# Reading the moving columns of the projections' products backward, with the activations' tiles shifted by 64, 128 and 192 bytes against the weights

## The chip, the cores and the metric

The kernel runs on one core of one Trainium2 chip. The metric is the device time of one execution in microseconds; for the kernel before it is the median of three runs. Names of engines follow the profile: PE is TensorE's matmul row, PEld its weight loads, DVE VectorE, ACT ScalarE, POOL GpSimd, SP the engine that issues most transfers.

## The reference, cut to what matters

Two layers of a hybrid block on 512 tokens of width 1024. Nearly all of the arithmetic is float32 matrix products:

```python
h = rms_norm(x, g_pre_mix);  proj = h @ w_in            # 1024 -> 7752 columns, split in q, k, v, ...
y_a = dsa_attention(q, k, v, qi, ki, wi)                # top-128 selection of keys, 8 heads
y_b = rg_lru(conv(xr), ...) * gelu(gr)
y_c = chunked_spatial_gating(gelu(zu), rms_norm(gelu(zv)), w_spatial, b_spatial)
merged = sum_n sigmoid(gate_logits_n) * (ys_n @ w_branch_n)
x = x + rms_norm(merged @ w_out)
f = square(relu(rms_norm(x) @ w_ffn_up)) @ w_ffn_down;  x = x + rms_norm(f)
ple = (p_i @ w_ple) * sigmoid(x @ w_ple_gate);          x = x + rms_norm(ple)
```

## The kernel before, in words

Activations lie transposed: channels on the 128 partitions, 512 tokens along a row, so that a tile has 512 float32 columns (2048 bytes a partition) and `D_MODEL` is eight tiles. To keep float32 precision each operand is split into a high and a low part of type float32r, and a product is the sum of three matmuls: high weights by high x, low weights by high x, high weights by low x (`mm3`, L296 to L299). A matmul of this kind loads 128 weight columns (the stationary operand, read from `wh` or `wl`) and then streams the moving columns (`xh`, `xl`, or the tiles `K`, `V`, `A`, `B`) through the array into a PSUM bank. In a profile's row `ps<-xh,wh` the first name behind the arrow is the moving operand and the second the weights.

`gemm` (L301) runs `mm3` over the contraction's tiles, so that one output tile of 1024 channels takes 24 matmuls. `gemm_arriving` (L338) is the same for stretches in which the moving tiles are still being made; its matmuls are at L355. `gemm_halves` (L323) calls `gemm` on halves of 256 columns. The other matmuls call TensorE directly and are not touched by the change: `tokens` (L589), the indexer's and the attention's (L657, L661, L671, L958), the float32 transposes through `ident` (L162, L433, L630, L944) and the sums of squares (L407).

The weights of one output tile come in one transfer of 512 KB into `wr`, ACT casts them into `wh` (L242), DVE subtracts to get `wl` (L243). Engines run their instructions in the order in which the Python program writes them; side chains (the indexer's selection, the recurrence, the attention's softmax) are woven in between by a model clock, `tick`, that counts planned microseconds of products.

Where tiles lie: a pool hands out addresses in the order in which its tags first appear, and `LEAD` shifts the first big tile. In the built program every tile that is named here starts at a multiple of 2048 bytes of its partition: `xh`, `xl`, `K`, `V`, `A`, `B`, `M`, `wh`, `wl` and `tmp` alike. A block of 128 weight columns is 512 bytes. So all moving and all weight reads of these products start at 0 modulo 256 bytes. `ident` is the one big moving operand that doesn't: it starts at 64 modulo 256.

Of the kernel before, what the change touches and what calls it, by code (L numbers as in the profile page):

```python
# [8 lines left out]
F32 = mybir.dt.float32  # L9
F32R = mybir.dt.float32r  # L10
# [9 lines left out]
KT = 8  # L20
# [30 lines left out]
def hybrid_block_kernel(ctx, tc, xT, pT, pos, vec, bsp, freq, w_in, w_tok, w_lru, w_sp, w_br, w_out, w_up, w_dn, w_ple, w_gate, out, depth=DEPTH, dbg=None):  # L51
    nc = tc.nc
    V, A, G, PE = nc.vector, nc.scalar, nc.gpsimd, nc.tensor

    cp = ctx.enter_context(tc.tile_pool(name="cp", bufs=1))
# [7 lines left out]
    def nm(p):  # L63
        uid[0] += 1
        return f"{p}_{uid[0]}"

    def tmp(dt=F32):
        return tp.tile([128, S], dt, tag="tmp", name=nm("tmp"), bufs=NTMP)
# [4 lines left out]
    def bank():  # L73
        return pp.tile([128, 512], F32, tag="ps", name=nm("ps"), bufs=8)

    def slot(tag, dt=F32, big=False):
        return cp.tile([128, 4, S] if big else [128, S], dt, tag=tag, name=nm(tag))
# [5 lines left out]
    def width(r):  # L83
        return r.stop - r.start
# [146 lines left out]
    def prep():  # L231
        i = nprep[0]
        nprep[0] += 1
        key, src = order[i]
        raw = wp.tile([128, 1024], F32, tag="wr", name=nm("wr"), bufs=3)
        nc.sync.dma_start(raw, src)
        if key[0] == "sp":
            r3 = raw.rearrange("p (g t) -> p g t", g=8)
            G.affine_select(out=r3, in_=r3, compare_op=ALU.is_ge, fill=0.0, base=0, pattern=[[0, 8], [1, 128]], channel_multiplier=-1)
        hi = wp.tile([128, 1024], F32R, tag="wh", name=nm("wh"), bufs=NWB)  # L240
        lo = wp.tile([128, 1024], F32R, tag="wl", name=nm("wl"), bufs=NWB)
        A.copy(hi, raw)  # L242
        V.tensor_sub(lo, raw, f32v(hi))  # L243
        prepared[key] = (hi, lo)

    def getw(key, ahead=LA):
        assert order[nget[0]][0] == key, (order[nget[0]][0], key)
        nget[0] += 1
        while nprep[0] < min(nget[0] + ahead, len(order)):
            prep()  # L250
        return prepared.pop(key)
# [33 lines left out]
    def tick(us):  # L285
        clk[0] += us
        run_later()
        run_tasks()
# [4 lines left out]
            tick(0.3)  # L293


    def mm3(ps, wh, wl, xh, xl, start, stop):  # L296
        PE.matmul(ps, wh, xh, start=start, stop=False)  # L297
        PE.matmul(ps, wl, xh, start=False, stop=False)  # L298
        PE.matmul(ps, wh, xl, start=False, stop=stop)  # L299

    def gemm(ps, w, xs, kk, c0=0, st=None, r=FULL):  # L301

# [7 lines left out]
    @contextmanager  # L310
    def ordered(last):

        cur = nc.cur_bb
        n0 = len(cur.bb.instructions)
        yield
        for i in cur.bb.instructions[n0:]:
            if i.engine in last:
                tc.add_manual_dep(i, last[i.engine], mybir.DependencyInfo(mybir.DependencyClass.NoSync, mybir.DependencyReason.DATA), reason="ordered")
            last[i.engine] = i.name
# [14 lines left out]
    def gemm_arriving(keys, xs, source, ranges, arrived=None, lag=LAG, tail=TAIL):  # L334


        n = len(keys)
        ws = [getw(key, 0) for key in keys[:-1]]  # L338
        pss = [bank() for _ in keys]
        last = {}  # L340
        for r in ranges:
            gen = source(r)
            for k in range(KT):
                with ordered(last):
                    next(gen)
                    todo = [(o, k) for o in range(len(ws))]
                    if len(ws) < n and k == lag:
                        ws.append(getw(keys[-1], 0))
                        todo += [(n - 1, q) for q in range(k + 1)]
                    if r is ranges[-1] and k >= KT - tail:  # L350
                        todo = [] if k < KT - 1 else [(o, q) for o in range(n) for q in range(KT - tail, KT)]
                    for i, (o, q) in enumerate(todo):
                        h3, l3 = [v.rearrange("p (k c) -> p k c", k=KT) for v in ws[o]]
                        for m in range(3):
                            PE.matmul(pss[o][:, r], (h3, l3, h3)[m][:, q], xs[q][m // 2][:, r], start=q == 0 and m == 0, stop=q == KT - 1 and m == 2)  # L355
                        if r is ranges[-1] and q == KT - 1 and o < n - 1:
                            prep()
                tick(0.65 * len(todo) * width(r) / S)
            if arrived is not None:
                arrived(r)  # L360
        while nprep[0] < nget[0] + LA:
            prep()
        return pss
# [84 lines left out]
    class Norm:  # L448
# [16 lines left out]
        def source(self, r):  # L465
            while r.start not in self.gens:
                tick(0.1)
            return self.gens[r.start]

    XS = [(slot(f"xh{k}", F32R), slot(f"xl{k}", F32R)) for k in range(KT)]  # L470

    def x_tiles(r, xs, g=None, st=None, ys=None, bc=None, gp=None, on_g=()):

        def updated(d):
            if ys is not None and d < KT:
                if gp is None:
                    V.tensor_mul(ys[d][:, r], ys[d][:, r], bc)
                else:  # L480
                    V.scalar_tensor_tensor(ys[d][:, r], ys[d][:, r], gp[:, d:d + 1], bc, op0=ALU.mult, op1=ALU.mult)
                (G if d in on_g else V).tensor_add(X[d][:, r], X[d][:, r], ys[d][:, r])  # L482

        updated(0)
        for d in range(KT):
            x = X[d][:, r]
            if xs is not None:
                hi, lo = [v[:, r] for v in xs[d]]
                if g is None:
                    A.copy(hi, x)  # L490
                else:
                    A.activation(hi, x, AF.Copy, scale=g[:, d:d + 1])  # L492
                if st is not None:
                    st.square(x, r)
            updated(d + 1)
            if st is not None:
                st.accumulate(r)
            if xs is not None:
                if g is None:
                    V.tensor_sub(lo, x, f32v(hi))  # L500
                else:
                    V.scalar_tensor_tensor(lo, x, g[:, d:d + 1], f32v(hi), op0=ALU.mult, op1=ALU.subtract)  # L502
            yield d
# [28 lines left out]
    for l in range(depth):  # L532
# [6 lines left out]
        if l == 0:  # L539
            st = Stats()  # L540

            def gen():
                tiles = x_tiles(FULL, XS, vc[:, V_PRE:V_PRE + 8], st)
                for k in range(KT):
                    first_parts(k)
                    yield next(tiles)
# [5 lines left out]
        rt = st.rt  # L552
        first = gemm_arriving([("in", l, f"xr{j}") for j in range(3)], XS, norm.source if l else lambda r: gen0, HALVES if l else (FULL,), st.row(D, R), 0, TAIL if l else 1)

        def proj(name, ahead=LA):
            ps = bank()
            gemm(ps, getw(("in", l, name), ahead), XS, KT)
            return ps
# [19 lines left out]
        def tokens(n, fn):  # L578
# [3 lines left out]
            for t0 in (0, 2):  # L582
                pss = [bank(), bank()]
                for k in range(KT):
                    wh, wl = [v[:, k % 2] for v in ws[k // 2]]
                    for t, ps in enumerate(pss, t0):
                        xh, xl = [v[:, t * 128:(t + 1) * 128] for v in XS[k]]
                        for i, (x, w) in enumerate(((xh, wh), (xl, wh), (xh, wl))):
# [13 lines left out]
        for j in range(4):  # L602
            ps = first[j]
# [7 lines left out]
            xh, xl = slot(f"B{j}", F32R), slot(f"B{4 + j}", F32R)  # L611
# [5 lines left out]
        ps = proj("ki")  # L617
# [28 lines left out]
        for j in range(4):  # L646
            ps = proj(f"qi{j}")
# [103 lines left out]
        for j in range(4):  # L751
            ps = proj(f"zu{j}")
# [16 lines left out]
        for j in range(4):  # L769
# [3 lines left out]
            for hf in range(2):  # L773
                ps = bank()
# [4 lines left out]
                for s in range(2):  # L779
                    r = slice(64 * s, 64 * s + 64)  # L780
# [55 lines left out]
        for j in range(4):  # L836
# [3 lines left out]
            xc, xh, xl = XC[j]  # L840
# [3 lines left out]
            r, i = tmp(), tmp()  # L844
# [165 lines left out]
        for j in range(4):  # L1010
            f = rope(proj(f"q{j}"))
            q2, ql = (slot(f"A{j}", F32R), slot(f"A{4 + j}", F32R)), tmp(F32R)
            for s in range(2):
                r, other = slice(64 * s, 64 * s + 64), slice(64 - 64 * s, 128 - 64 * s)
# [15 lines left out]
        for d in range(8):  # L1030
            if d % 2 == 0:
                w = getw(("br", l, 0, d // 2))
# [10 lines left out]
        def out_evac(d, r, ps):  # L1043
            st.add(ps, r)
            A.activation(Y[d][:, r], ps, AF.Copy, scale=col(V_POST + d))

        for d in range(5):
            ps = bank()
            gemm(ps, getw(("out", l, d)), M, KT)
            out_evac(d, FULL, ps)  # L1050
        norm = Norm(st, D, lambda r, bc: x_tiles(r, XS, vc[:, V_FFN:V_FFN + 8], st2, Y, bc, on_g=(1, 3, 5)))
        gemm_halves([("out", l, d) for d in (5, 6, 7)], M, lambda i, r, ps: out_evac(5 + i, r, ps), norm.complete)


        R = cp.tile([128, S], F32, tag="R", name=nm("R"))
        first = gemm_arriving([("up", l, 0, i) for i in range(4)], XS, norm.source, HALVES, st2.row(D, R))
        ps = bank()
        gemm(ps, getw(("up", l, 0, 4)), XS, KT)
# [51 lines left out]
        for c in range(2):  # L1110
            w = getw(("ple", l, c), ahead=1)
            if c == 1:
                bc = st3.rstd_bc()
            for i in range(4):
                ps = bank()
# [14 lines left out]
        for d in range(5):  # L1130
            if d < 4:
                ps = first[d]
            else:
                ps = bank()
# [95 lines left out]
```

## Time and profile before

| | |
|---|---|
| median of 3 runs (lowest to highest) | 1858.88 us (1858.13 to 1859.21) |
| the profiled execution's own time | 1859.11 us |
| its span, first to last instruction | 1857.4 us |
| PE busy | 1804.0 us, 97% of the span, 8798 matmuls |
| PEld busy | 1507.9 us, 81% |
| DVE, ACT, POOL busy | 1161.0, 800.9, 361.3 us |
| DMA | 167.77 MB, mean 90 GB/s |
| granted TensorE clock, mean | 0.99 |

A matmul's end is modelled in the profile and overlaps the next one, so that the pitch from start to start, not the duration in a row, tells what a matmul costs.

### The profile page before, as it was taken

Reading aid. Unit: us, or ns where it says so; the run is one execution under the profiler, and the core shown is the slowest. Engines: PE = TensorE matmul, PEld = TensorE weight load, DVE = VectorE, ACT = ScalarE, POOL = GpSimd, SP = SyncE. Lnnn points to the kernel's source line nnn. Section 1 sums busy time; section 2 is a strip of 40 time slices with the busy share of each in tenths; the row PEclk is TensorE's granted clock in tenths of the full one; section 3 lists DMA queues with packets and bytes.
Section 4 is the critical chain, followed back from the end, with each engine's and each line's share of the span. In section 5 each row is a group of like instructions: output and inputs, shape, how many; then the busy total and the mean of one; then the engine's idle time right before and its main releaser. Section 6 shows DMA issues by size and latency. Waiting matters only on the chain.

```text
span 1857.4 us, 22874 instructions
## 1 busy us (share of the span) xinstructions
PE 1804.0 (97%) x8798; PEld 1507.9 (81%) x8798; DVE 1161.0 (63%) x1939; ACT 800.9 (43%) x1292; POOL 361.3 (19%) x292
## 2 busy tenths in 40 slices
PE   8899999999999999999998999999999999999997
PEld 7787777888888888888887877877888888888886
DVE  6689986666386253533685999866563852545355
ACT  5466435564353231323554572455544432222233
POOL 3513212210140000003354141222003200000033
PEclk9999999999999999999999999999999999999998
DMA  5122222222223222232212122221222222222321
GB/s 172 63 91 90 87 97 84 76 78 82 80 91 103 100 93 102 91 114 91 89 60 97 66 93 92 102 80 69 91 80 91 91 91 102 92 101 94 111 80 58
DMA packets 49678, 167.77 MB, mean 90 GB/s; under 512 B 6048, under 2 KB 8864, under 8 KB 49568
## 3 DMA queue, kind: packets, MB, share of 16 engines
q1 hardware_dynamic: 47376, 163.64, 25.7%
q10 hardware_dynamic: 2192, 2.67, 0.4%
q8 instruction: 69, 1.13, 0.2%
q14 instruction: 41, 0.34, 0.1%
HBM read 164.19 MB, written 2.10 MB: 90 GB/s over the span
## 4 chain that ended last, share of the span: by engine, by line
PE 72%; DVE 14%; POOL 5%; issue 4%; ACT 4%; DMA 0%; SPq 0%; POOLq 0%; DVEq 0%; ACTq 0%
PE ps L297 20%; PE ps L299 20%; PE ps L298 20%; PE ps L589 4%; PE ps L355 4%; DVE wl L243 2%; DVE tmp L706 2%; DVE m L704 2%; POOL tmp L574 1%; POOL tmp L575 1%; PE ps L958 1%; POOL sacc L397 1%; POOL X L482 1%; PE ps L671 1%; DVE tmp L781 1%
## 5 line engine op out<-in xcount | busy, mean ns | idle before, releaser
L242 ACT CAST wh<-wr 128x1024 fp32r<-128x1024 f32 x303 | 316.7, 1049 | 453.2 <-PE ps L299 369.2
L243 DVE TENSOR_TENSOR wl<-wr,wh 128x1024 fp32r<-128x1024 f32 x303 | 386.0, 1278 | 190.7 <-ACT wh L242 189.9
L297 PE MATMUL ps<-xh,wh 128*128 128x512 f32 (+1 forms) x1296 | 502.2, 388 | 0.0
L298 PE MATMUL ps<-xh,wl 128*128 128x512 f32 (+1 forms) x1296 | 495.1, 382 | 3.0 <-DVE wl L243 3.0
L299 PE MATMUL ps<-xl,wh 128*128 128x512 f32 (+1 forms) x1296 | 495.4, 382 | 0.0
L397 POOL TENSOR_TENSOR sacc<-sacc,tmp 128x256 f32<-128x256 f32 (+1 forms) x99 | 109.7, 1109 | 893.7 <-issue 584.5
L299 PEld LDWEIGHTS ps<-xl,wh 128*128 128x128 f32 x1296 | 243.7, 188 | 48.2
L298 PEld LDWEIGHTS ps<-xh,wl 128*128 128x128 f32 x1296 | 244.0, 188 | 46.9 <-DVE wl L243 3.8
L297 PEld LDWEIGHTS ps<-xh,wh 128*128 128x128 f32 x1296 | 243.8, 188 | 45.5 <-issue 1.9
L299 PE MATMUL ps<-V,wh 128*128 128x512 f32 (+1 forms) x528 | 195.5, 370 | 0.0
L297 PE MATMUL ps<-K,wh 128*128 128x512 f32 (+1 forms) x432 | 158.2, 366 | 0.0
L298 PE MATMUL ps<-K,wl 128*128 128x512 f32 (+1 forms) x432 | 157.9, 365 | 0.0
L299 PE MATMUL ps<-B,wh 128*128 128x512 f32 x336 | 131.0, 390 | 0.0
L297 PE MATMUL ps<-A,wh 128*128 128x512 f32 x320 | 125.0, 391 | 0.0
L298 PE MATMUL ps<-A,wl 128*128 128x512 f32 x320 | 124.6, 389 | 0.0
L1089 DVE TENSOR_TENSOR M<-M,ps 128x512 f32<-128x512 f32 x48 | 33.0, 688 | 141.4 <-PE ps L299 141.4
L299 PEld LDWEIGHTS ps<-V,wh 128*128 128x128 f32 x528 | 99.5, 188 | 16.8
L1077 DVE TENSOR_TENSOR tmp<-ps,R 128x512 f32<-128x512 f32 x64 | 43.9, 691 | 108.4 <-PE ps L299 108.4
L355 PE MATMUL ps<-xl,wh 128*128 128x256 f32 (+1 forms) x264 | 88.2, 334 | 7.7 <-DVE xl L502 6.9
L297 PEld LDWEIGHTS ps<-K,wh 128*128 128x128 f32 x432 | 81.5, 189 | 13.2
L298 PEld LDWEIGHTS ps<-K,wl 128*128 128x128 f32 x432 | 81.5, 189 | 13.1
L355 PE MATMUL ps<-xh,wh 128*128 128x256 f32 (+1 forms) x264 | 86.5, 328 | 1.0 <-ACT xh L492 1.0
(237 smaller groups left out, 2738.5 us busy)
## 6 DMA issues: line engine op xcount, KB each, us to landing
wr<-in_w_in_dram SPq DMA_DIRECT2D x95, 512.0 KB, 3.2
wr<-in_w_up_dram SPq DMA_DIRECT2D x64, 512.0 KB, 3.2
wr<-in_w_dn_dram SPq DMA_DIRECT2D x64, 512.0 KB, 3.2
wr<-in_w_br_dram SPq DMA_DIRECT2D x24, 512.0 KB, 3.2
wr<-in_w_tok_dram SPq DMA_DIRECT2D x16, 512.0 KB, 3.2
wr<-in_w_out_dram SPq DMA_DIRECT2D x16, 512.0 KB, 3.2
wr<-in_w_gate_dram SPq DMA_DIRECT2D x16, 512.0 KB, 3.2
X<-in_xT_dram SPq DMA_DIRECT2D x8, 256.0 KB, 5.2
```

Source lines behind the costliest of these rows:

```text
L242: A.copy(hi, raw)
L243: V.tensor_sub(lo, raw, f32v(hi))
L297: PE.matmul(ps, wh, xh, start=start, stop=False)
L298: PE.matmul(ps, wl, xh, start=False, stop=False)
L299: PE.matmul(ps, wh, xl, start=False, stop=stop)
L355: PE.matmul(pss[o][:, r], (h3, l3, h3)[m][:, q], xs[q][m // 2][:, r], start=q == 0 and m == 0, stop=q == KT - 1 and m == 2)
L397: G.tensor_add(sacc[:, r], sacc[:, r], self.q[r.start, r.stop])
L589: PE.matmul(ps, x, w, start=k == 0 and i == 0, stop=k == KT - 1 and i == 2)
L704: V.max(m8, (sc if r == 0 else wk)[:, :n])
L706: V.match_replace(wk[:, :n], m8, (sc if r == 0 else wk)[:, :n], -3.0e38)
L1077: V.tensor_mul(t, ps, R)
L1089: V.tensor_add(F[d], F[d], ps)
```

## The change

A new helper `mm` hands TensorE both the moving operand and the output with a column step of -1, so that the last column is streamed first and lands in the last column of the bank: the same product in the same place. `mm3` and the matmuls of `gemm_arriving` call it. And `gap` puts four unused pieces of 64 bytes into the pool that holds the activations, and calls `slot` early for K, V, A and B so that they stand together. In the built program `xh` and `xl` then start at 64 modulo 256 bytes, K and V at 128, A and B at 192; `wh`, `wl`, `tmp`, `M` and `R` stay at 0.

```diff
+    def mm(ps, w, x, start, stop):
+
+        PE.matmul(ps[:, ::-1], w, x[:, ::-1], start=start, stop=stop)
+
     def mm3(ps, wh, wl, xh, xl, start, stop):
-        PE.matmul(ps, wh, xh, start=start, stop=False)
-        PE.matmul(ps, wl, xh, start=False, stop=False)
-        PE.matmul(ps, wh, xl, start=False, stop=stop)
+        mm(ps, wh, xh, start, False)
+        mm(ps, wl, xh, False, False)
+        mm(ps, wh, xl, False, stop)
...
-                            PE.matmul(pss[o][:, r], (h3, l3, h3)[m][:, q], xs[q][m // 2][:, r], start=q == 0 and m == 0, stop=q == KT - 1 and m == 2)
+                            mm(pss[o][:, r], (h3, l3, h3)[m][:, q], xs[q][m // 2][:, r], q == 0 and m == 0, q == KT - 1 and m == 2)
...
+    GAPS = (64, 64, 64, 64)
+
+    def gap(i):
+        if GAPS[i]:
+            cp.tile([128, GAPS[i] // 4], F32, tag=f"gap{i}", name=f"gap{i}")
+
+    gap(0)
     XS = [(slot(f"xh{k}", F32R), slot(f"xl{k}", F32R)) for k in range(KT)]
+    gap(1)
+    for n in ("K0", "K1", "V0", "V1"):
+        slot(n, F32R, True)
+    gap(2)
+    for n in range(8):
+        slot(f"A{n}", F32R)
+        slot(f"B{n}", F32R)
+    gap(3)
```

No engine's instructions change their order. What differs in the built program are waits on PE: 241 of its instructions wait for PE's own semaphore, where 90 did, because the first matmul into a bank now names the earlier matmul that last wrote it. On PE, at the start of an output tile of `w_out` in the first layer (`ps` is the bank, `K` and `V` the merged activations, the numbers behind the names are those of buffers), the kernel before has this order:

```order
L297 MATMUL ps_4263<-K_826_4057,wh_4142 128x512
L298 MATMUL ps_4263<-K_826_4057,wl_4143 128x512
L299 MATMUL ps_4263<-V_828_4059,wh_4142 128x512
L297 MATMUL ps_4298<-K_825_4056,wh_4182 128x512
L298 MATMUL ps_4298<-K_825_4056,wl_4183 128x512
L299 MATMUL ps_4298<-V_827_4058,wh_4182 128x512
```

and the changed kernel, at the same place, this:

```order
L298 MATMUL ps_4287<-K_846_4081,wh_4166 128x512
L298 MATMUL ps_4287<-K_846_4081,wl_4167 128x512
L298 MATMUL ps_4287<-V_848_4083,wh_4166 128x512
L298 MATMUL ps_4322<-K_845_4080,wh_4206 128x512 [waits PE_49]
L298 MATMUL ps_4322<-K_845_4080,wl_4207 128x512
L298 MATMUL ps_4322<-V_847_4082,wh_4206 128x512
```

Nothing has moved; the first matmul of the tile has a wait more. In each of the 241 places the matmul that is waited for stands at least 32 matmuls earlier in PE's order.

## Rows read from the trace of the kernel before

**Rows 1.** The page, parts 1 and 2: busy time, and 40 slices of the span.

```profile
PE 1804.0 (97%) x8798; PEld 1507.9 (81%) x8798; DVE 1161.0 (63%) x1939; ACT 800.9 (43%) x1292; POOL 361.3 (19%) x292
...
PE   8899999999999999999998999999999999999997
...
PEclk9999999999999999999999999999999999999998
```

**Rows 2.** Who waited for whom, PE alone: total us, times, longest us.

```profile
PE ps L589 <- DVE wl L243: 16.3, 6, 4.2
PE ps L355 <- DVE xl L502: 6.9, 8, 3.7
PE ps L298 <- DVE wl L243: 6.3, 4, 1.6
PE ps L958 <- ACT tmp L368: 3.9, 6, 2.1
```

**Rows 3.** Timeline of PE, 599.7 to 605.8 us: start, duration, matmul; one row a matmul.

```profile
599.72 0.39 PE L299 MATMUL ps<-xl,wh 128*128 128x512 f32 x1
599.95 0.39 PE L297 MATMUL ps<-xh,wh 128*128 128x512 f32 x1
600.18 0.39 PE L298 MATMUL ps<-xh,wl 128*128 128x512 f32 x1
...
605.84 0.39 PE L299 MATMUL ps<-xl,wh 128*128 128x512 f32 x1
```

**Rows 4.** Timeline of PE, 136.4 to 137.6 us, products of 256 columns.

```profile
136.40 0.28 PE L297 MATMUL ps<-wh,K 128*128 128x256 f32 x1
...
137.59 0.28 PE L298 MATMUL ps<-wh,K 128*128 128x256 f32 x1
```

**Rows 5.** Timeline of PEld at the same place as rows 3.

```profile
600.18 0.19 PEld L299 LDWEIGHTS ps<-xl,wh 128*128 128x128 f32 x1
600.41 0.19 PEld L297 LDWEIGHTS ps<-xh,wh 128*128 128x128 f32 x1
```

**Rows 6.** Timeline of PE at two groups of transposes, four and three.

```profile
294.11 0.60 PE L944 MATMUL ps<-ident,tmp 128*128 128x128 f32 x4
...
297.31 0.49 PE L944 MATMUL ps<-ident,tmp 128*128 128x128 f32 x3
```

**Rows 7.** Busy time over the whole span of L297, L298, L299, L355 alone, in that order.

```profile
0.00:1858.00 1858.00, 864.63 (x2256) 424.49 (x2256) 0.99 0.26 90
...
0.00:1858.00 1858.00, 855.53 (x2256) 424.81 (x2256) 0.99 0.26 90
...
0.00:1858.00 1858.00, 855.81 (x2256) 424.36 (x2256) 0.99 0.26 90
...
0.00:1858.00 1858.00, 136.31 (x792) 117.90 (x792) 0.99 0.26 90
```

**Rows 8.** Windows: span, busy us of PE, PEld, DVE, ACT, POOL; clock, DMA, GB/s.

```profile
139.00:232.00 93.00, 89.88 (x397) 73.85 (x396) 89.35 (x165) 51.15 (x63) 28.84 (x22) 1.00 0.26 88
1058.00:1180.00 122.00, 115.96 (x509) 95.05 (x508) 115.86 (x212) 59.37 (x77) 28.85 (x22) 1.00 0.27 91
530.00:900.00 370.00, 369.63 (x1684) 307.73 (x1683) 180.28 (x224) 114.15 (x146) 27.02 (x22) 1.00 0.28 96
1450.00:1800.00 350.00, 349.63 (x1583) 290.57 (x1582) 165.21 (x202) 106.28 (x133) 19.39 (x16) 1.00 0.29 100
```

**Rows 9.** Groups by line and form: the products of 256 columns at L355, L297, L298, L299.

```profile
L355 PE MATMUL ps<-xl,wh 128*128 128x256 f32 x176 | 52.7, 299 | 3.9 <-DVE xl L502 3.1
...
L355 PE MATMUL ps<-xh,wh 128*128 128x256 f32 x176 | 51.1, 290 | 0.0
L355 PE MATMUL ps<-xh,wl 128*128 128x256 f32 x176 | 50.4, 287 | 0.0
...
L297 PE MATMUL ps<-K,wh 128*128 128x256 f32 x96 | 27.5, 286 | 0.0
```

## The prediction

> **What bounds the kernel now.** I read the page first: PE is busy for 97% of the span, in every slice but the ends, at the full granted clock of 2.4 GHz (0.99 on the mean) [rows 1]. That share alone proves little, since the ends of matmuls are modelled, so the list of waits comes next. PE's waits that the profile can see add up to little: the four largest groups make 33.4 us of a span of 1857.4 us, all of them for freshly split weights or activations [rows 2]. In the two feed-forward stretches, 720 us together, PE is busy without a break while DVE and ACT are at half load or less [rows 8]. So the time is set by how fast PE goes from one matmul to the next, and the timeline of PE gives that pitch.
>
> Between 599.72 and 605.84 us stand 27 pitches of products of 512 columns: 6.12 us / 27 = 226.7 ns each [rows 3]. Products of 256 columns go at (137.59 - 136.40) / 10 = 119 ns [rows 4]. The 256 columns between the two cost 107.7 ns, 0.42 ns each, which is one cycle of the granted 2.4 GHz. By that cycle 512 columns are 213.3 ns and 256 are 106.7 ns; the excess is 13.4 ns in the one and 12.3 ns in the other. It does not grow with the columns: it is paid once a matmul. What else happens once a matmul is the weight load of the next one, and the timeline of the loads shows it starting together with the running product (600.18 us in both views) [rows 3, 5]. So the moving stream and the weight stream read their operands at the same time for the first part of each product, and the excess is where a change of direction and of addresses could act. This is an inference: no row of this kernel shows products with other addresses or another direction.
>
> The Trainium skill has a rule against this reading: "TensorE: Matmul & The Clock Gate", section "Step-by-step: what each phase is for", says that PE reads the moving operand and the weights through two independent ports, so that loading the next weights takes nothing from the running product. By it addresses would not matter, and the kernel would stay at its time. The same page ("Back-to-back issue gap") gives about 216 ns for 512 columns; here the trace shows 226.7 ns, so that about 11 ns of what I see is not in the page's sum. The first of these is a rival below.
>
> **The change part by part.**
>
> *The backward, shifted products.* How many: the three lines of `mm3` have 2256 matmuls each and `gemm_arriving` has 792 [rows 7], 3 x 2256 + 792 = 7560. What one can save: at most the whole excess, 13.4 ns. At least nothing if the excess is something else, and less than nothing if the new pattern collides more (priced under the rivals). Between the ends I look for the nearest row in which a moving stream starts at another address than the weights modulo 256. There is one: the transposes, whose moving operand `ident` starts at 64. Four of them span 0.60 us and three 0.49 us, so one costs 0.11 us [rows 6], and this is with a load of 128 weight columns for each. A product of 256 columns, which also has one load, takes 119 ns. The transposes are float32 and only 128 columns, so this is a distant relative; but it says that a load with a shifted moving stream can pass in about 110 ns, 9 ns below the product's pitch. I take 9 ns of the 13.4 as saved, for 512 and 256 columns alike since the excess is alike. 7560 x 9 ns = 68.0 us.
>
> *What of it is not on the path.* In two stretches, 139 to 232 and 1058 to 1180 us, DVE is busy for 89.35 of 93.0 and 115.86 of 122.0 us (the indexer's selection and the gates) [rows 8]. PE runs 397 + 509 matmuls there, which would give back 8.2 us, and DVE has 3.65 + 6.14 us to spare. DVE is next late there; its queue is in program order and PE waits for `wl` from it. I take half as lost, 4.1 us. The 792 matmuls of `gemm_arriving` wait for their own operands, 6.9 us in total [rows 2]; where a tile arrives late, a faster product only waits longer. 792 x 9 ns = 7.1 us, half of it lost, 3.5 us. In the rest the weights' chain has room: in the feed-forward stretches DVE is at 180.28 of 370.0 us and ACT at 114.15 [rows 8], so that a 4% faster PE does not make them late.
>
> *The new waits.* 151 more instructions on PE wait for PE's own semaphore. Behind a waiting matmul stands all of PE. But what is waited for lies 32 or more matmuls back, over 7 us at 226.7 ns, and a matmul's result is out within 0.4 us of its start [rows 3]. Cost: nothing. The cover is that distance; if the wait were for the matmul just before, the 0.39 us of duration less the pitch, 0.16 us, would be paid 151 times, 24 us.
>
> *The moved tiles.* ACT, DVE and POOL read and write x, K, V, A and B at other addresses, with the same shapes and in the same order. No row shows what 64 bytes do to them; I price it at nothing, because these engines have slack except in the two stretches above. The products that still read forward (`tokens`, attention, indexer) now have weights at 64 to 192 bytes from the moving tiles. They are 8798 - 7560 = 1238 matmuls, transposes included [rows 1, 7]; the sign is open, and even 9 ns on all of them is 11 us either way. I take 0.
>
> *The sum.* 68.0 - 4.1 - 3.5 = 60.4 us. From the profiled execution's own time, 1859.1 us, that is 1798.7 us; the median of the runs lies 0.2 us lower, so 1798.5 us.
>
> **The rivals.** A difference under 0.2% (3.7 us) is no change that a measurement of this kernel can tell.
>
> *The excess is not a collision.* If the 13 ns are a fixed cost of exchanging weights, neither direction nor address matters. For it: it is the same at 256 and 512 columns [rows 3, 4], as a fixed cost would be. Against it: a transpose, which exchanges weights too, passes in 0.11 us [rows 6]. Time: 1859 us. The two-port rule of the Trainium skill's page named above would have it so.
>
> *The moving stream gets stuck behind the weights' stream.* This ends on the slower side. The products read 128 columns in 53 ns; the load of 128 weight columns takes about 110 ns [rows 6]. If the load reads in the same direction as the backward stream and has the right of way, the faster moving stream comes up from behind and can't pass: it crawls for what is left of the load. At worst it loses 110 - 53 = 57 ns, 44 ns more than now, 330 us in all; if it catches up half way, some 15 ns more than now, 7560 x 15 ns = 113 us, and the kernel takes about 1972 us. It decides from the point at which the new excess is over 13.4 ns. For it: the shift is only 64 to 192 bytes, 16 to 48 columns, and the difference in speed is large. Against it: the stream would have to be barred from passing, and no product in these rows is held by more than 13.4 ns.
>
> *Writing a bank backward is slow.* The output is written backward too. The Trainium skill, "PSUM — Partial Sum Buffer", section "Specifications (TRN2)", says that an access pattern that isn't contiguous slows matmuls significantly; it does not say whether backward counts as such. As a mechanism here: if each result column takes two cycles rather than one, 512 columns take 427 ns for 227 and 256 take 213 for 119. 1200 of the 7560 have 256 columns (3 x 176 at L355 and 672 at the other three lines, of whose seven groups of 96 one is shown) [rows 9], so 6360 x 0.200 + 1200 x 0.094 = 1385 us more, 3244 us. Against it: neighbours still follow each other, two by two. No row here shows a backward write.
>
> **How the numbers follow.** The forecast, a gain by a smaller excess, has 0.70; no effect 0.12; the stuck stream, or a milder loss of its kind, 0.14; the slow write 0.04. Within the first, the saving a matmul runs from 4 ns (30 us less about 3, 1832 us) to 12 ns (91 us less about 10, 1778 us); that is the likeliest case's own range, 1776 to 1832 us. A range that leaves out the two slower cases and a little of the first holds 8 in 10: 1776 to 1863 us. The chances: faster by over 0.2%: 0.70; within: 0.12; slower: 0.18.
>
> **What would show it right or wrong.** In the timeline of PE at the same feed-forward place, 27 pitches should take about 5.9 us instead of 6.12 (217.7 ns), and products of 256 columns about 110 ns. If x (shift 64), K and V (128) and A and B (192) differ, three pitches will stand in the feed-forward stretch, by the name of the moving tile. DVE's share in 139 to 232 us should rise towards all of it, and PE's waits for `wl` with it. Unchanged pitches with an unchanged time are the first rival; pitches above 227 ns the second; pitches near 427 ns the third. PE's waits for PE should stay out of the list of waits. I am wrong in size if the pitch falls but PE's waits grow by more than the 7.6 us given above.

## The result, and the profile after

The change makes the kernel slower. The median of four runs is 1884.78 us (1883.88 to 1886.15) against 1858.51 us (1857.65 to 1859.21) for the kernel before on the same chip: a ratio of 1.0142, with a 95% interval of 1.0125 to 1.0160. The prediction said 1798.5 us. The profiled execution's span is 1882.2 us, 24.8 us more than before.

The page after, parts 1 and 2, answers to [rows 1]. PE has the same 8798 matmuls and is still busy in every slice, at the same clock; the engine that was the bound is still the bound, and does the same work more slowly.

```profile
PE 1840.9 (98%) x8798; PEld 1507.6 (80%) x8798; DVE 1158.5 (62%) x1939; ACT 800.4 (43%) x1292; POOL 358.8 (19%) x292
...
PE   8899999999999999999998999999999999999997
...
PEclk9999999999999999999999999999999999999998
```

The timeline of PE in the feed-forward stretch, at the place of [rows 3], gives the pitch. From 599.89 to 606.19 us are 27 pitches, 6.30 us: 233.3 ns each, where it was 226.7 ns. The forecast was 217.7 ns. So the sign of the effect on a product is wrong, not only its size.

```profile
599.66 0.40 PE L298 MATMUL ps<-xl,wh 128*128 128x512 f32 x1
599.89 0.40 PE L298 MATMUL ps<-xh,wh 128*128 128x512 f32 x1
600.13 0.40 PE L298 MATMUL ps<-xh,wl 128*128 128x512 f32 x1
...
606.19 0.40 PE L298 MATMUL ps<-xh,wh 128*128 128x512 f32 x1
```

Products of 256 columns hardly change. At the place of [rows 4] the first row below and the last stand 21 products apart (the profile joins two neighbours in some rows between): 2.51 us / 21 = 119.5 ns, against 119 ns before. In these rows the spatial gating's weights, in `wl`, are the moving operand, and the tile `K` is loaded.

```profile
135.60 0.28 PE L298 MATMUL ps<-wl,K 128*128 128x256 f32 x1
...
138.11 0.28 PE L298 MATMUL ps<-wl,K 128*128 128x256 f32 x1
```

The list of PE's waits answers to [rows 2]. The wait of `tokens` for `wl` (L589 before, L609 now; the helper moves the lines) went from 16.3 to 13.4 us, that of the products for `wl` from 6.3 to 1.9 us, that of `gemm_arriving` for `xl` (now a part of the group at L298, since both kinds call `mm`) from 6.9 to 6.0 us. A slower PE waits less for others.

```profile
PE ps L609 <- DVE wl L243: 13.4, 6, 4.2
PE ps L298 <- DVE xl L522: 6.0, 9, 2.8
...
PE ps L298 <- DVE wl L243: 1.9, 2, 1.0
```

Where in the program is the time lost? The transposes of the attention stand at both ends of a long piece of it. Their group, first in the kernel before and then in the changed one, gives the start of the first and of the last of 160 (behind "first and last" in the view: 294.1 to 1357.1 us).

```profile
L944 PE MATMUL ps<-ident,tmp x160: 270/272/275, 294.1 to 1357.1; 128*128 128x128 f32 x160
```

```profile
L964 PE MATMUL ps<-ident,tmp x160: 271/272/274, 291.4 to 1369.8; 128*128 128x128 f32 x160
```

At the first transpose the changed kernel is 2.7 us ahead, at the last 12.7 us behind, at the end 24.8 us behind. PE's matmuls stand in the same order in both kernels, so that each can be set against its other self. Done for all of them, the lag is -1.5 us at 465 us, 10.2 us at 930 us, 13.7 us at 1395 us. From 465 to 930 and from 1395 to the end, which hold the two feed-forward stretches, it grows by 11.7 and 11.1 us; all of the rest gives 2.0 us. The same pairing sorts the time from each matmul's start to the next one's ("close" is a pitch under the columns at 2.4 GHz plus 32 ns in both traces):

| matmuls | number | before, us | after, us | difference, us |
|---|---|---|---|---|
| `mm3`, 512 columns, close | 5970 | 1357.4 | 1394.2 | +36.8 |
| `mm3`, 512 columns, with a gap behind | 126 | 51.0 | 43.3 | -7.6 |
| `gemm_arriving`, 512 columns, close | 246 | 55.8 | 57.4 | +1.6 |
| `gemm_arriving`, 512 columns, with a gap behind | 18 | 12.2 | 10.2 | -2.0 |
| `tokens`, close | 336 | 76.5 | 78.3 | +1.8 |
| `tokens`, with a gap behind | 48 | 35.6 | 30.1 | -5.5 |
| 256 columns of both kinds, close | 1117 | 133.6 | 133.9 | +0.2 |
| all others | | | | -0.5 |

So the products lose about 40 us, and 15 us come back in gaps, most of them waits for other engines, which did not move. A few of the 15 us are differences between two executions: in the run below that writes backward but reads forward, where no product is slower, the same pairing gives -2.2 us for the gaps of `gemm_arriving`, and from -2.7 to +2.8 us for those of `tokens` at single places. A pitch decides only where nothing else is waited for, and that is above all in the feed-forward stretches: from 530 to 900 us the lag grows by 10.2 us, from 1450 to 1800 us by 9.7 us.

The windows answer to [rows 8]. Between 139 and 232 us DVE is as busy as before, 89.31 us of 93: no slack came free there. In the feed-forward stretches PE gets fewer records into the same time (1640 where it had 1684 in the first).

```profile
139.00:232.00 93.00, 91.90 (x393) 73.45 (x392) 89.31 (x164) 50.02 (x62) 28.70 (x22) 1.00 0.29 91
530.00:900.00 370.00, 369.67 (x1640) 299.89 (x1639) 174.36 (x216) 109.65 (x140) 25.08 (x21) 1.00 0.29 96
```

### The profile page after: what moved, and what is told of

Read it like the earlier page. It is cut to its first block, busy times and chain, and to the rows that moved or that the text cites. A ratio compares the mean times of both kernels' runs of the same rounds, so it can differ in the third digit from the quotient of the medians.

```text
span 1882.2 us, 22927 instructions
## 1 busy us (share of the span) xinstructions
PE 1840.9 (98%) x8798; PEld 1507.6 (80%) x8798; DVE 1158.5 (62%) x1939; ACT 800.4 (43%) x1292; POOL 358.8 (19%) x292
## 4 chain that ended last, share of the span: by engine, by line
PE 72%; DVE 14%; POOL 5%; issue 4%; ACT 4%; DMA 0%; SPq 0%; POOLq 0%; ACTq 0%; DVEq 0%
PE ps L298 65%; PE ps L609 4%; DVE wl L243 2%; DVE tmp L726 2%; DVE m L724 2%; POOL tmp L594 1%; POOL tmp L595 1%; PE ps L978 1%; POOL sacc L401 1%; POOL X L502 1%; PE ps L691 1%; DVE tmp L801 1%; DVE M L630 1%; PE ps L964 1%; PE ps L677 0%
## 5 line engine op out<-in xcount | busy, mean ns | idle before, releaser
L298 PE MATMUL ps<-xl,wh 128*128 128x512 f32 (+1 forms) x1560 | 591.1, 379 | 6.6 <-DVE xl L522 6.0
L298 PE MATMUL ps<-xh,wh 128*128 128x512 f32 (+1 forms) x1560 | 596.3, 382 | 0.8 <-ACT xh L512 0.8
L298 PE MATMUL ps<-xh,wl 128*128 128x512 f32 (+1 forms) x1560 | 588.8, 378 | 0.3
L298 PEld LDWEIGHTS ps<-xl,wh 128*128 128x128 f32 x1560 | 294.1, 189 | 69.4 <-DVE xl L522 10.6
L298 PEld LDWEIGHTS ps<-xh,wh 128*128 128x128 f32 x1560 | 294.4, 189 | 57.0 <-issue 1.9
L298 PEld LDWEIGHTS ps<-xh,wl 128*128 128x128 f32 x1560 | 294.5, 189 | 54.6 <-DVE wl L243 1.1
L298 PE MATMUL ps<-V,wh 128*128 128x512 f32 (+1 forms) x624 | 225.1, 381 | 0.0
L298 PE MATMUL ps<-K,wh 128*128 128x512 f32 (+1 forms) x432 | 161.2, 373 | 0.0
L298 PE MATMUL ps<-K,wl 128*128 128x512 f32 (+1 forms) x432 | 160.8, 372 | 0.0
L298 PE MATMUL ps<-B,wh 128*128 128x512 f32 x416 | 158.6, 400 | 0.0
L298 PE MATMUL ps<-A,wh 128*128 128x512 f32 x384 | 142.6, 398 | 0.0
L298 PEld LDWEIGHTS ps<-V,wh 128*128 128x128 f32 x624 | 117.1, 188 | 23.9
L298 PE MATMUL ps<-A,wl 128*128 128x512 f32 x320 | 127.1, 397 | 0.0
L298 PEld LDWEIGHTS ps<-K,wl 128*128 128x128 f32 x432 | 81.2, 188 | 15.7
L298 PEld LDWEIGHTS ps<-B,wh 128*128 128x128 f32 x416 | 78.2, 188 | 19.3 <-PE ps L681 0.6
L298 PEld LDWEIGHTS ps<-K,wh 128*128 128x128 f32 x432 | 81.2, 188 | 15.5
L298 PEld LDWEIGHTS ps<-A,wh 128*128 128x128 f32 x384 | 72.0, 188 | 17.8 <-ACT A L372 0.5
```

The source lines that it names most:

```text
L298: PE.matmul(ps[:, ::-1], w, x[:, ::-1], start=start, stop=stop)
```

## The experiments

The change has three parts that can be taken apart: the read is backward, the write is backward, the moving tiles are shifted. My theory after the result was that the direction in which the moving operand is read is what costs. The rivals were that the shift costs, that the backward write costs, and that the moving stream is held by the weight load beside it. Four small kernels hold series alone: a series is 48 products in a row from one tile. Its pitch can be read from the start of a series and of the next, and the means in the tables leave out the first 16 products, in which PE still waits for other work in some series. Each kernel of series was timed once. In two of them the series that is repeated at the end comes within 0.1 ns of its twin; in the other two the first series still holds waits behind its 16th product (228.4 and 228.0 ns), and the repeat is used.

**Backward, without the shift.**

```diff
-    GAPS = (64, 64, 64, 64)
+    GAPS = (0, 0, 0, 0)
```

> The changed kernel with all four gaps at 0: backward reading, all parts at 0 modulo 256 bytes from the weights. Theory 1 (direction: the backward stream runs the same way as the weight load and is held by it, whatever the shift): pitch of 512 columns near 233 ns as in the changed kernel, time near 1885 us. Theory 2 (the shifts cost, the direction does nothing): pitch 226.7 ns, time near 1859 us. If the shift spares something of the backward reading's cost, the time is above 1885 us.

Measured: 1882.1 us, ratio 1.0124 (1.0109 to 1.0139). In its timeline of PE the two rows below are 27 pitches apart, 6.30 us, 233.3 ns each. Nearly all of the loss is there with no shift at all.

```profile
599.99 0.40 PE L298 MATMUL ps<-xh,wh 128*128 128x512 f32 x1
...
606.29 0.40 PE L298 MATMUL ps<-xh,wh 128*128 128x512 f32 x1
```

**Shifted, forward.**

```diff
-        PE.matmul(ps[:, ::-1], w, x[:, ::-1], start=start, stop=stop)
+        PE.matmul(ps, w, x, start=start, stop=stop)
```

> The changed kernel with forward reading and writing, the shifts of 64, 128 and 192 bytes kept. Theory 1 (direction): pitch 226.7 ns, time near 1859 us. Theory 2 (shifts): pitch 233 ns, near 1885 us. If both matter, the pitches differ by the name of the moving tile.

Measured: 1874.53 us, ratio 1.0081 (1.0064 to 1.0098). The timeline of PE in the feed-forward stretch of this kernel has 29 pitches between its first row here and its last: 6.63 us / 29 = 228.6 ns, for x at 64 bytes.

```profile
599.64 0.39 PE L298 MATMUL ps<-xh,wl 128*128 128x512 f32 x1
...
606.27 0.39 PE L298 MATMUL ps<-xh,wh 128*128 128x512 f32 x1
```

Products from K and V (128 bytes) go at some 232 ns, from A and B (192 bytes) at 233. So each half of the change alone makes the kernel slower, and the two do not add: 1.24% and 0.81% alone, 1.42% together. A backward read costs about the same at the four places that these kernels use; a forward read is cheapest at 0, where the kernel before had its tiles.

**The pitch by shift and direction.** A kernel of series alone: the weights stay, the moving tile starts at a multiple of 16 bytes.

```diff
+                    x = mv[:, at:at + n]
+                    if mb:
+                        x = x[:, ::-1]
+                    PE.matmul(o, w, x, start=k == 0 and m == 0, stop=k == 7 and m == 2)
```

> Not the reference's computation: it copies x to the output and, beside it, runs series of 48 products of float32r with 128 weight columns, moving columns at 16 shifts modulo 256 bytes, forward and backward, reading backward alone, writing backward alone, with 256 columns, and with moving and weights shifted together. Theory 1 (same direction as the load): forward near 227 ns at all shifts, backward near 233 ns, reading backward alone 233 ns, writing backward alone 227 ns, 256 columns near 120 ns both ways. Theory 3 (the backward write of the bank costs): writing backward alone 233 ns, reading backward alone 227 ns. If the shift matters, the pitch varies over the 16 shifts by up to 13 ns; then the best shift and direction give a kernel faster than both.

Measured, ns a product of 512 columns, by shift in bytes (forward at 0 is the repeat at the kernel's end; the seven shifts left out lie between 231.0 and 234.3 forward, and at 233.3 or 233.4 backward):

| | 0 | 16 | 32 | 64 | 112 | 128 | 192 | 208 | 240 |
|---|---|---|---|---|---|---|---|---|---|
| both forward | 226.7 | 231.5 | 233.3 | 228.9 | 231.3 | 232.3 | 233.4 | 234.5 | 226.7 |
| both backward | 233.4 | 233.4 | 233.3 | 233.3 | 233.4 | 236.6 | 233.3 | 233.4 | 236.6 |
| read backward alone | 233.4 | | | 233.4 | | 233.4 | 233.3 | | |
| write backward alone | 226.6 | | | 229.0 | | 232.7 | 233.3 | | |

The groups by tile show it: a row's last pair of times are the start of the first and of the last product that read `wh`. The backward read at 0 starts at 374.5 us and the backward write at 385.7 us, 11.2 us / 48 = 233 ns; from there to the next series it is 10.9 us / 48 = 227 ns.

```profile
L97 PE MATMUL read_bwd_nil<-mv,wh x32: 396/398/398, 374.5 to 385.5; 128*128 128x512 f32 x32
...
L97 PE MATMUL write_bwd_nil<-mv,wh x32: 388/389/399, 385.7 to 396.4; 128*128 128x512 f32 x32
...
L97 PE MATMUL read_bwd_sixtyfour<-mv,wh x32: 396/398/398, 396.6 to 407.6; 128*128 128x512 f32 x32
```

With a forward read the write's direction costs nothing at any shift: its row follows that of the forward read. Beside a backward read it adds 3.2 ns at 128 (236.6 against 233.4) and nothing at 0, 64 and 192; why at 128 is not shown. The read's direction costs 6.7 ns at 0 and takes most of the effect of the shift away. Weights and moving tile shifted together (64, 128, 192) give 226.7 forward and 233.3 backward again, so what counts forward is the one against the other. Products of 256 columns, forward: 120.0 at 0, 117.8 at 64, 118.7 at 128, 113.3 at 192; backward 118.2, 120.0, 120.1, 117.7. That is why they stand still in the kernel.

**Only the write backward, in the kernel.** It has no shift, and since only the columns' order in the bank is turned, its values are not the reference's.

```diff
-    GAPS = (64, 64, 64, 64)
+    GAPS = (0, 0, 0, 0)
...
-        PE.matmul(ps[:, ::-1], w, x[:, ::-1], start=start, stop=stop)
+        PE.matmul(ps[:, ::-1], w, x, start=start, stop=stop)
```

> No gaps; moving columns read forward, only the bank written backward (each product's columns land reversed, so the values differ from the reference's). If the direction of the read alone costs: pitch 226.7 ns, time within 0.2% of before. If the backward write costs inside the kernel after all: pitch near 233 ns and about 1882 us.

Measured: 1857.83 us over ten runs, ratio 0.9995 (0.9986 to 1.0004): no change. In its timeline of PE the two rows below are 27 pitches apart, 6.12 us, 226.7 ns each.

```profile
599.81 0.39 PE L298 MATMUL ps<-xh,wh 128*128 128x512 f32 x1
...
605.93 0.39 PE L298 MATMUL ps<-K,wh 128*128 128x512 f32 x1
```

**Backward in the feed-forward stretches alone, and outside them alone.** Both without a shift; a flag is set where the stretch begins and reset behind it (the other way round in the second kernel).

```diff
+        if back[0]:
+            PE.matmul(ps[:, ::-1], w, x[:, ::-1], start=start, stop=stop)
+        else:
+            PE.matmul(ps, w, x, start=start, stop=stop)
...
+        back[0] = True
...
+        back[0] = False
```

> No gaps; backward reading and writing only in the feed-forward's products (up and down), forward in all others. Theory a (the other stretches absorb a slower PE in waits that get shorter): about 2900 products of 512 columns at 6.6 ns more, 19 us, all of it on the path: near 1878 us. Theory b (every product costs the same share of the 23 us): 2900 of 6360, so about 10.5 us, near 1869 us.

> No gaps; backward in all products but the feed-forward's. Theory a: some 3400 products of 512 columns at 6.6 ns more, 23 us of PE time, of which the waits before L609 and for freshly split operands give back 15 us or more: 1862 to 1867 us. Theory b: 1871 us.

Measured: inside, 1876.36 us, ratio 1.0093 (1.0078 to 1.0108); outside, 1864.1 us over ten runs, ratio 1.0028 (1.0019 to 1.0038). The products lose about the same in both, 19.0 and 18.7 us by the pairing used above. Inside, all but some 2 us of it reaches the end; outside, 4.9 us does. The lists of PE's waits say why. Inside, those for `wl` are what they were in [rows 2], 16.4 and 6.3 us:

```profile
PE ps L614 <- DVE wl L243: 16.4, 6, 4.2
PE ps L303 <- DVE wl L243: 6.3, 4, 1.6
```

Outside, they have shrunk, to 13.9 and 2.2 us, and by the pairing 11.6 us in all come back from gaps (L614 is `tokens` here, L301 and L303 are the backward and the forward call in `mm`):

```profile
PE ps L614 <- DVE wl L243: 13.9, 6, 4.2
...
PE ps L301 <- DVE wl L243: 2.2, 4, 0.9
```

So the same slower product costs the kernel nearly all of its loss in one place and about a quarter of it in the other.

**Shorter weight loads.** Series again, with 32, 64, 96 and 128 weight columns.

```diff
+                    w = (wh, wl, wh)[m][:, 128 * (k % 7) + woff:128 * (k % 7) + woff + cols]
```

> Not the reference's computation: it copies x to the output and runs series of 48 products beside it. Weight loads of 32, 64, 96 and 128 columns under products of 512, forward at shift 0 and 128 bytes, and backward; shifts of 4, 8 and 12 bytes around 0; and products of 256 columns forward at 16 shifts. If the excess over 213.3 ns is the moving stream held by the load, it shrinks with the load's length (13.4 ns to about 3 to 4 with 32 columns, backward 20 ns to about 5). If it is a fixed cost of exchanging weights, the pitch is the same for all four lengths. Products of 256 columns: the lowest pitch near a shift of 192, 113 ns.

The groups of PEld show that the load did get shorter: 108 ns (the mean behind the comma) with 32 weight columns, 188 with 128.

```profile
L97 PEld LDWEIGHTS load_all_bwd<-mv,wh 128*128 128x128 f32 x32 | 6.0, 188 | 1.5
...
L97 PEld LDWEIGHTS load_thirtytwo_bwd<-mv,wh 128*32 128x32 f32 x32 | 3.5, 108 | 4.0
```

The groups by tile of PE show that the products didn't: 217.7 to 228.9 us is one series backward with the short load, 11.2 us / 48 = 233 ns.

```profile
L97 PE MATMUL load_thirtytwo_bwd<-mv,wh x32: 395/395/400, 217.7 to 228.7; 128*32 128x512 f32 x32
...
L97 PE MATMUL load_sixtyfour_fwd<-mv,wh x32: 387/390/397, 228.9 to 239.7; 128*64 128x512 f32 x32
```

Backward the pitch is 233.4, 233.3, 233.3, 233.3 ns for 32, 64, 96, 128 weight columns; forward at 0 it is 231.7, 229.9, 230.0, 226.6, and forward at 128 bytes 230.6, 231.3, 231.5, 233.5. An excess that is paid while the load runs would shrink with the load. Backward it does not move. Forward the load matters by up to 5 ns, but with no one sign: at 0 the full load has the lowest pitch, at 128 bytes the highest. In none of the three rows does the excess come near the 3 to 5 ns that were expected of a load of 32 columns. The theory on which the prediction rested falls here.

**Other operands.** One kernel of series: two-byte operands, a moving operand that repeats one column, weights that repeat one column, every second column, 64 rows.

```diff
+                    if wconst:
+                        w = wts[m % 2][0:rows, at:at + 1].to_broadcast([rows, 128])
...
+                    x = mov[0:rows, at:at + n * step:step]
+                    if const:
+                        x = mov[0:rows, at:at + 1].to_broadcast([rows, n])
```

> Not the reference's computation: it copies x to the output and runs series of 48 products beside it, 512 columns where nothing else is said. Theory 1b (two streams of 4-byte operands meet in the memory, early in the load): with a moving operand of one repeated column, or weights of one repeated column, nothing is walked through and the pitch falls to about 216 ns; with 2-byte operands, half the bytes, it falls below 226.7 ns in both directions and the difference of direction shrinks. Theory 4 (a fixed cost of exchanging weights that only happens to differ by direction): all of these keep 226.7 forward and 233.3 backward. Operands on 64 rows alone, the same weights or the same moving tile every time: no change by either. Low parts shifted against high parts: a mean of the pitches of the shifts that meet, by the first table, so none under 226.7 ns. Columns from 192 to 448: the same excess at each number by theory 4; by theory 1b it may change with the number, since the end of one stream sets where the next load meets it.

| 512 columns | forward | backward |
|---|---|---|
| as in the kernel | 226.7 | 233.4 |
| two-byte operands (moving and weights), four shifts | 215.8 | 215.8 |
| one moving column repeated, four shifts | 216.8 | |
| one weight column repeated | 231.6 | 233.3 |
| 64 rows for 128 | 226.7 | 233.3 |
| the same weights and the same moving columns each time | 226.7 | 233.4 |
| every second column | 453.2 | |

In the timeline of PE 48 two-byte products in each direction stand in one row each. From the one start to the other it is 10.37 us / 48 = 216 ns.

```profile
26.32 10.53 PE L109 MATMUL half_word_fwd_nil<-mb,wb 128*128 128x512 bf16 x48
36.69 10.52 PE L109 MATMUL half_word_bwd_nil<-mb,wb 128*128 128x512 bf16 x48
```

Most of the excess is there only if the moving stream walks through four-byte columns: repeat one moving column and 10 of the 13.4 ns are gone, with the same weight loads (below, 47 pitches in 10.2 us, 217 ns); halve the bytes of both operands and 11 are. One weight column repeated takes nothing away: backward it changes nothing, forward it adds 4.9 ns.

```profile
L109 PE MATMUL one_column_sixtyfour<-mv,wh x32: 378/378/379, 119.6 to 129.8; 128*128 128x512 f32 x32
```

Two kinds of series are not in the table. With the direction turned at every second product the mean is 233.3 ns, as with all of them backward, so that the 6.7 ns are not a cost of each backward product by itself. With only some of the low parts shifted against the high parts it is 226.7 to 233.2 ns, none below the kernel's.

Every second column doubles the time of a product (the series starts at 184.3 and the next at 206.2 us, 21.9 us / 48 = 456 ns with its first products):

```profile
L109 PE MATMUL step_two<-mv,wh x32: 616/630/649, 184.3 to 205.6; 128*128 128x512 f32 x32
...
L109 PE MATMUL rows_half_fwd<-mv,wh x32: 386/386/492, 206.2 to 217.0; 64*128 64x512 f32 x32
```

**Once a product, or by the column?** The last series: 224 to 512 columns, forward at four shifts and backward at 0.

```diff
+        for q, v in ((0, "nil"), (28, "onetwelve"), (48, "oneninetytwo"), (60, "twoforty")):
+            series(f"columns_{w}_{v}", q, n=n)
+        series(f"columns_{w}_bwd", n=n, back=True)
```

> As in the pitch table, the kernel's work is left out: x is copied to the output and series of 48 products from one tile are timed, so only the pitches mean something. Here the columns a product run from 224 to 512 in steps of 32, forward at shifts of 0, 112, 192 and 240 bytes and backward at 0. By the cycle of 0.4167 ns the columns alone take 93.3 ns at 224 and 213.3 ns at 512. Theory A, a fixed cost a product: the lowest pitch over the shifts lies 13.3 ns above the columns at every length (133.3 at 288, 160.0 at 352, 186.7 at 416, 213.3 at 480). Theory B, a cost that grows with what the moving stream walks through: the lowest pitch is the columns by 17/16 (127.5 at 288, 155.8 at 352, 184.2 at 416, 212.5 at 480), with 6.7 or 13.3 ns more where a product starts badly. Backward by A: 20 ns above the columns at each length, by B: 17/16 and 6.7 ns more. A step of two columns with 256 of them walks through as many bytes as 512: by A 120 ns and what the step costs, by B 226.7 ns forward and 233.3 ns backward. Backward at 4, 8 and 12 bytes: 233.3 ns if the phase doesn't matter backward, above 236 ns if it does.

| columns | 256 | 288 | 320 | 352 | 384 | 416 | 448 | 480 | 512 |
|---|---|---|---|---|---|---|---|---|---|
| at 0.4167 ns each | 106.7 | 120.0 | 133.3 | 146.7 | 160.0 | 173.3 | 186.7 | 200.0 | 213.3 |
| lowest of four shifts, forward | 113.3 | 131.7 | 146.5 | 159.9 | 173.3 | 186.6 | 202.1 | 213.3 | 226.6 |
| backward at 0 | 118.3 | 133.3 | 146.7 | 162.3 | 177.7 | 191.1 | 206.8 | 220.0 | 233.3 |

From 320 columns on the lowest forward excess is 13.2 to 13.3 ns at every length but 448 (15.4), so it is paid once a product there, as theory A has it; at 256 columns it can be half of that. What backward at 0 adds to this lowest pitch grows with the length from 320 on: 0.2 ns at 320, 2.4 at 352, 4.4 to 4.7 from 384 to 448, 6.7 at 480 and 512. Below, it does not follow that line: 5.0 ns at 256, 1.6 at 288. Neither theory is right as a whole. With a step of two, 256 columns take 230.1 ns forward (below, 47 pitches in 10.8 us) and 233.3 backward, about what 512 neighbours take, as B has it: the stretch of memory that is walked through counts, not the columns alone.

```profile
L109 PE MATMUL step_two_half<-mv,wh x32: 391/409/418, 466.9 to 477.7; 128*128 128x256 f32 x32
```

Backward at 4, 8 and 12 bytes gives 235.5, 236.7 and 240.1 ns, so that the shift does matter there, by up to 6.8 ns.

No version was found that beats both kernels. No series that walks through 512 four-byte columns went under 226.6 ns, which the kernel before has; a shift of 192 would save 6.7 ns on products of 256 columns and cost 6.7 on those of 512, and the same tiles serve both, the long ones far more often [rows 7, 9].

## Why the prediction was wrong

**The step that failed** is the one that chose a saving: "I take 9 ns of the 13.4 as saved". The saving is -6.6 ns at 512 columns (226.7 to 233.3) and nothing at 256. The value came from the transposes [rows 6], the one row with another address; they are float32 of 128 columns, and the prediction called them a distant relative. The series show that products of 192 and of 224 columns both stand at 111.5 to 111.8 ns, in either direction: at such lengths the pitch no longer follows the columns. The 0.11 us of a transpose of 128 columns is most likely this same floor, which says nothing about the stream; no series had 128 columns, so that this is argued and not shown. A row that another limit sets can't price this one.

**The inference under it** was right in one half. The excess is paid once a product, as was read from two lengths [rows 3, 4]; the lengths from 320 to 512 bear it out for columns that stand side by side (with a step of two it fails). That it is what the weight load takes from the stream is wrong: a load of a quarter of the columns (108 ns for 188), and weights of one repeated column, leave the backward pitch where it was and do not lower the forward one at 0. With it falls the promise that another direction or address could free the stream.

**The count and the path.** 7560 matmuls were priced alike; only the 6360 of 512 columns changed. Of what the waits take up, 7.6 us were foreseen, at half of two terms; by the first table the gaps moved by about 15 us. In the two stretches in which DVE is nearly always busy, 139 to 232 and 1058 to 1180 us, `mm3` lost 5.3 us and its gaps gave back 4.0, more than the half that was assumed. The gaps of `gemm_arriving` gave back no more than they do where no product is slower. The waits of `tokens`, which gave back 5.5 us (about 3 of them may be a difference between executions), had no term, though their 16.3 us stood first in [rows 2]. DVE's share between 139 and 232 us was to rise with a faster PE, and with a slower one it did not fall: DVE sets the time there, as was said. The feed-forward stretches, named as those in which PE alone sets the time, made 19.9 of the 24.8 us.

**The rivals.** "The moving stream gets stuck behind the weights' stream" has the right sign, at half its price or less (6.6 ns for 15), and the wrong mechanism by the run with shorter loads (it also took a load for 110 ns, from the transposes, where [rows 5] records 0.19 us). "The excess is not a collision" is wrong in its fixed cost of exchanging weights, since one repeated moving column goes at 216.8 ns with the same loads, and wrong in what it drew from it: direction and address matter. The two-port rule, in the section "Step-by-step: what each phase is for" of the Trainium skill's page "TensorE: Matmul & The Clock Gate", was cited for this rival; backward, the runs agree with it, since neither the load's length (233.3 to 233.4 ns) nor its columns (233.3 ns) change a product; forward, the offset between the two operands does change it (226.7 to 238.4 ns), which independent ports alone would not explain. "Writing a bank backward is slow" is refuted twice (0.9995 in the kernel, 226.6 ns in the series).

**What held.** The new waits of PE for PE cost nothing: no such pair stands in the list of PE's waits. The moved tiles cost `tokens`, which still reads forward with its weights now shifted, 1.8 us, where I took 0 within 11 us either way.

**What stays open** is where the 6.7 ns of a backward read arise, why half of the products read backward are enough for them, and why they grow between 320 and 512 columns. The runs place them in the moving read (233.4 ns with the read backward alone), find no such difference with two-byte operands, and exclude the bank's direction at 0, the load's length and the weights' addresses; they don't show the mechanism. Forward, the shift modulo 256 isn't the whole of it either: at 240 bytes the pitch was 226.7 ns in one kernel and 236.5 in another whose products went through the tiles in another order.

## What to carry to other kernels

Before a change that should make every product of a kernel a little faster, measure the product alone, 48 in a row, at the shape in question; a row of another shape can be set by another limit and then says nothing, not even a sign. A constant excess per instruction does not tell its cause: shorten the suspect (here the load) and see if the excess shrinks. And multiply a change of pitch only over the stretches in which the engine waits for nobody; elsewhere the waits take it up, in a loss as in a gain.

## What the runs showed of the hardware that was not expected

- Products of 512 columns of float32r go at 226.7 ns at best, two-byte ones at 215.8. The Trainium skill's page "TensorE: Matmul & The Clock Gate" gives 518 cycles for 512 columns taken by themselves, without the next load ("Back-to-back issue gap"), which is 215.8 ns at 2.4 GHz: the runs, with a load for each product, agree with it for two-byte operands, and for four-byte ones only if a single column is repeated (216.8).
- A backward write into a bank is free beside a forward read (226.6 ns at 0). A backward read of the moving operand is not (233.4 ns), and it takes away most of what the address would do.
- A shift of 4 bytes against the weights costs more than any multiple of 16 bytes (238.4 ns forward, at most 234.5 for those in the first kernel of series); it is 232.9 ns at 8 bytes and 228.9 at 12.
- Every second four-byte column costs twice the time, 453.2 ns. The page "SBUF — State Buffer" of the Trainium skill says, in "Door 1: The DMA port swizzle (why `[64,N]` ≈ `[32,N]`)", that two accesses to a line of 16 bytes are enough for full bandwidth. A step of two leaves two of them, and this read lost half of its speed.
- A load of 32, 64, 96 and 128 weight columns is recorded with 109, 134, 161 and 188 ns (forward).
